# Order of copies, casts and held products in a decoder trunk on one core

## The chip, the cores and the metric

The kernel runs on one core of a Trainium2 chip. The metric is the device time of the whole kernel in microseconds (us), as the median of several runs. The core's engines are named as in the profile: PE (TensorE, matmuls; PEld is its weight load), DVE (VectorE), ACT (ScalarE), POOL (GpSimd) and SP (SyncE, which here only issues transfers).

## What is computed

A two-layer decoder trunk on 512 tokens with 16 learned ones put in front: 528 tokens of width 1024 in float32. Layer 0 mixes with retention (four heads), layer 1 with gated linear attention (GLA, four heads); each mixer stands between two half-step SwiGLU FFNs of inner width 2816.

```python
def rmsnorm(x, g):
    xf = x.astype(jnp.float32)
    y = xf * lax.rsqrt(jnp.mean(xf * xf, axis=-1, keepdims=True) + EPS)
    return (y * g).astype(x.dtype)

def swiglu(x, w_in, w_out):
    gate, up = jnp.split(x @ w_in, 2, axis=-1)
    return (jax.nn.silu(gate) * up) @ w_out
...
    h = jnp.concatenate([meta, x], axis=1)
    for i in range(DEPTH):
        j = i // N_MIXERS
        h = h + 0.5 * swiglu(rmsnorm(h, norm_ffn1[i]), ffn1_w_in[i], ffn1_w_out[i])
...
```

Then the mixer is added (`retention` for i = 0, `gla` for i = 1), then the second FFN, and after both layers a last `rmsnorm` and the first 16 tokens are dropped. `retention` projects to q, k, v and a gate, turns q and k by rotary angles, and runs chunks of 64 tokens with a decaying state.

## The kernel before

**Stages.** The activations stay on the chip, channels on partitions and tokens in two halves of 264. The stages run in turn: FFN f10, retention, FFN f20, FFN f11, GLA, FFN f21. Each FFN has its inner channels in groups: plain gate and up products of a few channels first (tiles `pf20g`, and so on), then per pair of inner tiles a gate unit `g` and an up unit `u`, and after each group the out units `o`, which add to the residual `x`.

**A product.** Matrices are split into a high and a low part, and each product of a 128x128 weight block with 264 tokens is three matmuls (`mm3`, L483 to L485): high weight by high activations, high weight by low, low weight by high.

**A unit.** Two output tiles by two token halves are not made with eight block products but with seven, named a11, s1, s2, a12, s4, s3, a22, on sums and differences of weights and activations. Each is 12 matmuls (9 where three gated tiles make a group). Their results land in three PSUM places: X takes a11, s2, s3 and a22 in the order that the unit has, Q takes a12, Z takes s1 and s4 (Q and Z are one tile, `QZ`). ACT copies X or Z away after s1 (L714), a11 (L716) and s2 (L720); after s3 DVE reads X for the result `c22`, after s4 it reads QZ for `row1`, and after a22 it or ACT reads X for `c21`. In a unit called `rqkk` (keys of a retention head) c22 is L1300 and row1 L1297; in an out unit c22 ends with L1037.

**Three orders of the seven.** A unit is by default held: its last product a22 isn't issued with the unit but kept in `W.held`, and runs when the next unit has begun or when `W.get` is asked for something that the plan doesn't have next (`settle`). So s4 stands before s3 and another unit's products before a22. `LAST` is for units that aren't held, with s3 before s4 and a22 at the end. `FIRST` is the order of an FFN's first unit.

```python
    UNIT = ("a11", "s1", "s2", "a12", "s4", "s3", "a22")
    LAST = ("a11", "s1", "s2", "a12", "s3", "s4", "a22")
    FIRST = ("s1", "s2", "a12", "a11", "s4", "s3", "a22")
```

**Weights.** The plan (`plan_ffn`, `plan_ret` and others) lists all weight pieces in order. SP loads them into `raw` and `pair` tiles; POOL issues transfers that add into `pair` (L151, L153). Sums for s2 and s4 are made by DVE (L191, L193). Then each piece is split: ACT casts `whi` (L184), DVE subtracts to get `wlo` (L185). `hook`, called after each of a unit's products, calls `W.fetch`, which splits up to AHEAD = 4 pieces beyond the one taken. The scheduler that sets the engines' final orders may move these further ahead: `urgent` gives what stands in it a head start of 300 instructions, and `issue_after` holds an instruction behind another.

**Activations of an FFN.** `renorm` splits the sums of the normed activations for the first units (`split`, L516, tiles `uhf`, `ulf`); `evac` takes a gate product with L905 (times the norm) and L906 (silu). `hidden` makes the gated tiles' high parts `hf` (L516).

**What a step does, in its order:** the products, `W.free`, `hook`, and only then the copy or the result.

Of the kernel before, what the change touches and what calls it, by code (L numbers as in the profile page):

```python
# [19 lines left out]
KD = D // P  # L20
# [5 lines left out]
NF = 22  # L26
# [42 lines left out]
class Weights:  # L69
# [11 lines left out]
    def __init__(self, tc, ctx, raw_bufs=7, pair_bufs=3, bufs=7):  # L81
        self.nc, self.tc = tc.nc, tc

        self.behind = None
# [75 lines left out]
    def _split(self, upto):  # L160
        V = self.nc.vector
        while self.split < min(upto, len(self.plan)):
# [17 lines left out]
            with ExitStack() as order_:  # L180
                if self.behind and i < self.FRONT:
                    for ins in self.behind:
                        order_.enter_context(self.tc.issue_after(ins.ins))
                act = self.nc.scalar.copy(hi[:, :n], raw)  # L184
                dve = V.tensor_sub(lo[:, :n], raw, hi[:, :n].bitcast(F32))  # L185
                self.newest = act, dve
# [79 lines left out]
def trunk(ctx, tc, a):  # L266
# [30 lines left out]
    def plan_ffn(w_in, w_out, layer, which, last=False, late=False):  # L297
        first = True
        for kind, a_, b_ in ffn_steps(last, late):
# [11 lines left out]
            elif kind == "i":  # L311
                W.add_unit(key, w_in[layer, o], w_in[layer, o + 1], first,
                           last and b_ == LAST_GROUPS[1][0], last or (a_, b_) != ("u", NF - 2))
# [374 lines left out]
    def unit_steps(key, name, order, halves, ks, rhs, places, row1, c22, c21, behind=None, done=None):  # L688
# [8 lines left out]
        def step(q):  # L697
            if not started:
                hold["X"], hold["QZ"], hold["ab"], hold["s"] = places()
            X, QZ, ab, s_ = [hold[i] for i in ("X", "QZ", "ab", "s")]  # L700
            what, into = WITH[q]
            to = {"X": X, "Q": QZ[:, 0], "Z": QZ[:, 1]}
            w = W.get(key + (q,))
            turn = ks(what)
            for k in turn:
                with tc.issue_after(behind.ins) if behind else ExitStack():
                    ends["unit"] = mm3(to[into], *W.at(w, k * P), *rhs(what, k), k == turn[0] and into not in started,
                                       k == turn[-1], skip_group_check=True)
            started.add(into)
            W.free(w)  # L710
            hook()
            with urgent():
                if q == "s1":
                    S.copy(s_[:, 0], to["Z"])  # L714
                elif q == "a11":
                    S.copy(ab[:, int(first)], X)  # L716
                    if first:
                        V.tensor_sub(ab[:, 0], ab[:, 1], s_[:, 1])
                elif q == "s2":
                    S.copy(s_[:, 1] if first else ab[:, 1], X)  # L720
                elif q == "s3":
                    c22(X, s_[:, 0])
                elif q == "s4":
                    row1(ab, QZ)
                elif q == "a22":
                    c21(X)
# [11 lines left out]
    def unit(key, name, halves, ks, rhs, place, row1, c22, c21, behind=None, done=None, hold=True, first=False):  # L738
# [8 lines left out]
        *steps, last = unit_steps(key, name, W.order(key, first, hold), halves, ks, rhs, places, row1, c22, c21, behind, done)  # L747
# [36 lines left out]
    def ffn(which, layer, halves, gcol, u, feed, late=False):  # L784
# [7 lines left out]
        with tc.tile_pool(name=f"h_{me}", bufs=1) as hp, tc.tile_pool(name=f"t_{me}", bufs=1) as tp, \  # L792
# [47 lines left out]
            def renorm():  # L840
                for h, r0, r1 in ((1, a0, a1), (0, a0, a1), (1, b0, b1)):
# [58 lines left out]
            def evac(f, outs):  # L900

                sg = tmp.tile([P, T], F32, tag="sg", name=f"sg{me}{f}")
                with urgent():
                    for o, view in outs["g"]:
                        V.tensor_mul(view(sg), o, view(rb))  # L905
# [73 lines left out]
            def unit_u(f, g, first):  # L979
# [7 lines left out]
                def row1(ab, qz):  # L987
# [3 lines left out]
                    V.tensor_mul(o, o, pair(g[0], halves))  # L991
                    if last:
                        hidden(f, y[0], 0)

# [11 lines left out]
                def done():  # L1006
                    if f < NPL:
                        todo.append((f, y[0]))
                    elif not last:
# [3 lines left out]
                     place_of[0], row1, c22, c21, None, done, not last, first)  # L1013

            def unit_o(gi, d, behind):
# [29 lines left out]
                unit((which, layer, "o", gi, d), f"{me}o{gi}{d}", halves, ks, rhs, place_of[0], row1, c22, c21, behind)  # L1045
# [3 lines left out]
            for n, (kind, a_, b_) in enumerate(steps):  # L1049
# [23 lines left out]
                elif kind == "i":  # L1073
                    if a_ == "g":
                        g = unit_g(b_, first)
                        if todo:
                            with behind(renormed):
                                hidden(*todo.popleft())
                    else:
# [3 lines left out]
                        unit_u(b_, g, first)  # L1083
                    first = False
# [152 lines left out]
    def retention(u, feed):  # L1237
        with tc.tile_pool(name="retp", bufs=1) as rp, tc.tile_pool(name="wmore", bufs=2) as wp, psum_pool(4) as pp:
# [48 lines left out]
            def head(h):  # L1287
                qk = {}

                def rope_pair(s):  # L1290
# [30 lines left out]
                    unit(("rqk", j), f"rqk{s}{h}", HALVES, rows4_odd, rhs_u, place, row1, c22, c21, None, done)  # L1321
# [978 lines left out]
```

## Time and profile before

| | us |
|---|---|
| median of 3 runs | 2027.35 |
| lowest and highest run | 2026.77, 2835.27 |
| profiled execution | 2025.93 |
| its span, first to last instruction | 2024.2 |
| mean granted PE clock in it | 0.998 |

Rows of the profile's groups give engine, operation, tiles (out<-in), count, busy time, mean ns of one, and idle time before with what ended most of it. Rows of a list of waits give what waited, for what, total us, times, the longest. Rows of a timeline give start and duration in us, and in brackets the idle time before and what ended it. Rows of windows give busy time per engine with instruction counts, then the granted clock, DMA share and GB/s. The lines themselves stand in the prediction where they are used.

### The profile page before, as it was taken

Reading aid. Unit: us, or ns where it says so; the run is one execution under the profiler, and the core shown is the slowest. Engines: PE = TensorE matmul, PEld = TensorE weight load, DVE = VectorE, ACT = ScalarE, POOL = GpSimd, SP = SyncE. Lnnn points to the kernel's source line nnn. Section 1 sums busy time; section 2 is a strip of 40 time slices with the busy share of each in tenths; the row PEclk is TensorE's granted clock in tenths of the full one; section 3 lists DMA queues with packets and bytes.
Section 4 is the critical chain, followed back from the end, with each engine's and each line's share of the span. In section 5 each row is a group of like instructions: output and inputs, shape, how many; then the busy total and the mean of one; then the engine's idle time right before and its main releaser. Section 6 shows DMA issues by size and latency. Waiting matters only on the chain.

```text
span 2024.2 us, 43485 instructions
## 1 busy us (share of the span) xinstructions
PE 2000.5 (99%) x16575; PEld 1967.0 (97%) x16575; DVE 1793.7 (89%) x3302; ACT 1192.0 (59%) x2427; POOL 209.9 (10%) x181
## 2 busy tenths in 40 slices
PE   9999999999999999999999999999999999999998
PEld 9999999999999999999999999999999989999998
DVE  8989999978787889989999998999897968999896
ACT  5656566554555465656666665666645545666664
POOL 1011111010101000111111011111001000111110
PEclk9999999999999999999999999999999999999999
DMA  7576877354645532776876477777515341687772
GB/s 228 137 203 172 205 192 183 106 163 119 164 120 147 135 111 74 181 204 159 212 187 166 127 184 192 180 198 177 183 64 126 103 139 58 166 214 179 183 192 68
DMA packets 176113, 318.87 MB, mean 158 GB/s; under 512 B 17568, under 2 KB 40736, under 8 KB 175904
## 3 DMA queue, kind: packets, MB, share of 16 engines
q1 hardware_dynamic: 133856, 237.04, 35.6%
q0 software_dynamic: 40896, 75.51, 23.4%
q10 hardware_dynamic: 1152, 3.55, 0.6%
q8 instruction: 130, 2.13, 0.4%
q14 instruction: 79, 0.65, 0.1%
HBM read 311.76 MB, written 4.26 MB: 156 GB/s over the span
## 4 chain that ended last, share of the span: by engine, by line
PE 80%; DVE 13%; issue 2%; ACT 2%; DMA 1%; POOL 0%; SPq 0%; DVEq 0%; POOLq 0%; ACTq 0%
DVE wlo L185 4%; PE po_r L484 1%; PE po_r L483 1%; PE po_r L485 1%; ACT whi L184 1%; PE lv L1820 1%; PE Xf11u L483 1%; PE Xf21o L483 1%; PE Xf11u L484 1%; PE Xf21o L485 1%; PE Xf11u L485 1%; PE Xf21o L484 1%; PE Xf21u L483 1%; PE Xf11g L484 1%; PE Xf11g L483 1%
## 5 line engine op out<-in xcount | busy, mean ns | idle before, releaser
L184 ACT CAST whi<-raw 128x512 fp32r<-128x512 f32 (+1 forms) x893 | 531.4, 606 | 436.3 <-DVE raw L193 160.7
L185 DVE TENSOR_TENSOR wlo<-raw,whi 128x512 fp32r<-128x512 f32 (+1 forms) x893 | 589.4, 668 | 105.1 <-ACT whi L184 91.1
L184 ACT CAST whi<-pair 128x512 fp32r<-128x512 f32 (+1 forms) x304 | 183.3, 604 | 67.4 <-ACT su L716 10.7
L185 DVE TENSOR_TENSOR wlo<-pair,whi 128x512 fp32r<-128x512 f32 (+1 forms) x304 | 201.3, 663 | 13.2 <-ACT whi L184 12.3
L153 POOL DMA_DIRECT2D pair<-in_f_in x73 | 89.0, 1220 | 713.3 <-DVE wlo L185 331.3
L193 DVE TENSOR_TENSOR raw<-raw,raw 128x512 f32<-128x512 f32 (+1 forms) x146 | 97.3, 667 | 3.3
L191 DVE TENSOR_TENSOR raw<-pair,raw 128x512 f32<-128x512 f32 (+1 forms) x146 | 97.0, 665 | 3.5 <-DVE wlo L185 0.8
L153 POOL DMA_DIRECT2D pair<-in_f_out x44 | 53.5, 1216 | 352.8 <-DVE wlo L185 125.7
L484 PE MATMUL po_r<-ogl,whi 128*128 128x264 f32 x256 | 71.3, 278 | 0.0
L483 PE MATMUL po_r<-ogh,whi 128*128 128x264 f32 x256 | 71.2, 278 | 0.0
L485 PE MATMUL po_r<-ogh,wlo 128*128 128x264 f32 x256 | 71.2, 278 | 0.0
L153 POOL DMA_DIRECT2D pair<-in_ret_in x20 | 24.4, 1222 | 317.7 <-DVE wlo L185 189.8
L965 ACT ACTIVATE gf<-gf 128x528 f32<-128x528 f32 (+1 forms) x36 | 23.2, 644 | 50.2 <-DVE gf L964 50.2
L483 PE MATMUL Xf10o<-hf,whi 128*128 128x264 f32 x176 | 49.5, 281 | 1.0 <-DVE x L1037 0.7
L483 PE MATMUL Xf20o<-hf,whi 128*128 128x264 f32 x176 | 49.2, 280 | 1.0 <-DVE x L1037 0.7
L483 PE MATMUL Xf11o<-hf,whi 128*128 128x264 f32 x176 | 49.2, 280 | 0.3 <-ACT hf L516 0.3
L484 PE MATMUL Xf10o<-hf,whi 128*128 128x264 f32 x176 | 49.1, 279 | 0.0
L484 PE MATMUL Xf20o<-hf,whi 128*128 128x264 f32 x176 | 49.0, 279 | 0.0
L484 PE MATMUL Xf11o<-hf,whi 128*128 128x264 f32 x176 | 49.0, 279 | 0.0
L485 PE MATMUL Xf10o<-hf,wlo 128*128 128x264 f32 x176 | 48.9, 279 | 0.0
L485 PE MATMUL Xf11o<-hf,wlo 128*128 128x264 f32 x176 | 48.8, 278 | 0.0
L485 PE MATMUL Xf20o<-hf,wlo 128*128 128x264 f32 x176 | 48.8, 278 | 0.0
(1182 smaller groups left out, 8605.2 us busy)
## 6 DMA issues: line engine op xcount, KB each, us to landing
raw<-in_f_in SPq DMA_DIRECT2D x277, 256.0 KB, 3.5
pair<-in_f_in SPq DMA_DIRECT2D x150, 256.0 KB, 4.9
pair<-in_f_in POOLq DMA_DIRECT2D x73, 512.0 KB, 7.6
raw<-in_f_out SPq DMA_DIRECT2D x80, 256.0 KB, 3.3
raw<-in_ret_in SPq DMA_DIRECT2D x76, 256.0 KB, 2.9
raw<-in_f_out SPq DMA_DIRECT2D x72, 192.0 KB, 3.0
pair<-in_f_out SPq DMA_DIRECT2D x48, 256.0 KB, 4.8
pair<-in_f_out POOLq DMA_DIRECT2D x24, 512.0 KB, 6.0
```

Of the source, the lines that this page charges most:

```text
L153: nc.gpsimd.dma_start(t, aps[2].unsqueeze(1).broadcast_to([P, 2, n]), accum_op=ALU.add)
L184: act = self.nc.scalar.copy(hi[:, :n], raw)
L185: dve = V.tensor_sub(lo[:, :n], raw, hi[:, :n].bitcast(F32))
L191: V.tensor_add(s2, self.tiles[c][:, 1], self.tiles[c, "a11"])
L193: V.tensor_add(raw, raw, s2)
L483: nc.tensor.matmul(ps, lhsT=lh, rhs=rh, start=start, stop=False, **kw)
L484: nc.tensor.matmul(ps, lhsT=lh, rhs=rl, start=False, stop=False, **kw)
L485: return nc.tensor.matmul(ps, lhsT=ll, rhs=rh, start=False, stop=stop, **kw)
L965: S.activation(o, o, AF.Silu, scale=-1.0)
L1820: nc.tensor.matmul(ps[:, j, J * P:J * P + n], lhsT=Kt[:, j, J * P:(J + 1) * P], rhs=q, start=(J == 0), stop=(J == 3), skip_group_check=True)
```

## The change

No operation is added or removed; only orders change, in four parts.

**Unheld units ahead of plain products.** The last out unit of f10, f20 and f11 (`feed` given, d = KD - 2 in the last group), the last up unit of f21, and the k units of retention's heads 1 to 3 run in the order LAST, with a22 at their own end. The plan gives the weights in that order too.

**Copies ahead of casts.** For s1, a11 and s2 the copy is now issued before `hook`, and the casts and subtractions of that fetch are held behind the copy (`W.after`).

**First units.** All splits of `renorm` but the first pair stand behind DVE's last product of the gate (`ends["sg"]`), but not in f10 (`late`); the first `hidden` stands behind the copies.

**First out unit of the last group, in two parts.** a11 and s1 run with all gated tiles but the newest, then a11 and s1 with the newest (`parted`).

The core of the diff:

```diff
+                if self.after:
+                    order_.enter_context(self.tc.issue_after(self.after.ins))
                 act = self.nc.scalar.copy(hi[:, :n], raw)
...
                 if kind == "o":
-                    W.add_unit(key, w_out[layer, b_, :, c], w_out[layer, b_ + 1, :, c], False, last and a_ == 0, True)
+                    W.add_unit(key, w_out[layer, b_, :, c], w_out[layer, b_ + 1, :, c], False, last and a_ == 0,
+                               last or (a_, b_) != (len(GROUPS) - 1, KD - 2))
...
-                    W.add_unit(("rqk", j), a["ret_in"][j], a["ret_in"][j + 1], hold=True)
+                    W.add_unit(("rqk", j), a["ret_in"][j], a["ret_in"][j + 1], hold=j < 8)
...
+            if part is not None:
+                late = max(turn)
+                turn = [k for k in turn if k != late] if part == 0 else [late]
...
+        def step(q, part=None):
+            products(q, part)
+            if part == 0:
+                return
+            if q in ("s1", "a11", "s2") or final and q == "s4":
+                W.after = results(q)
+                if first:
+                    ends["copy"] = W.after
+                hook()
+                W.after = None
+            else:
+                hook()
+                results(q)
             if q == "a22" and done:
                 done()
...
+        if parted:
+            (q0, q1), rest = order[:2], order[2:]
+            return [lambda q=q, part=part: step(q, part) for part in range(2) for q in (q0, q1)] + \
+                [lambda q=q: step(q) for q in rest]
         return [lambda q=q: step(q) for q in order]
...
-                        renormed[:] = split(*u.block(k, k + 2, int(r0 == b0)), normed[j][:, :, 1 - h, r0:r1])
+                        with behind([ends["sg"]] if n and not late else []):
+                            renormed[:] = split(*u.block(k, k + 2, int(r0 == b0)), normed[j][:, :, 1 - h, r0:r1])
...
                         if todo:
-                            with behind(renormed):
+                            with behind(renormed + ([ends["copy"]] if first else [])):
                                 hidden(*todo.popleft())
...
                 unit((which, layer, "i", "u", f), f"{me}u{f}", halves, rows4, rhs_in,
-                     place_of[0], row1, c22, c21, None, done, not last, first)
+                     place_of[0], row1, c22, c21, None, done, f + 2 != NF, first, last)
...
-                unit((which, layer, "o", gi, d), f"{me}o{gi}{d}", halves, ks, rhs, place_of[0], row1, c22, c21, behind)
+                unit((which, layer, "o", gi, d), f"{me}o{gi}{d}", halves, ks, rhs, place_of[0], row1, c22, c21, behind,
+                     hold=not feed or (gi, d) != (len(groups) - 1, KD - 2),
+                     parted=bool(feed) and (gi, d) == (len(groups) - 1, 0))
```

What it does to the engines' instructions is shown at three places; line numbers are those of each kernel's own text, and the number behind a name tells tiles apart.

At the first unit of f20, ACT's queue before the change (`su` is the place of the unit's copies, from `QZf20u` after s1 and from `Xf20u` after s2):

```order
L184 CAST whi430_11063<-raw227_10717 128x512
L184 CAST whi431_11082<-pair90_10148 128x512
L516 CAST uhf20_10316<-unf200_10679 128x2x264
L184 CAST whi432_11103<-raw229_10793 128x512
L516 CAST uhf20_10316<-unf201_10825 128x2x264
L906 ACTIVATE sgf203_11032<-sgf203_11032 128x528
L184 CAST whi433_11120<-pair91_10299 128x512
L714 COPY su7_11050<-QZf20u2_11049 128x264
L516 CAST hf200_11301<-unf200_10679 128x3x264
L720 COPY su7_11050<-Xf20u2_11048 128x264
```

The same place after it:

```order
L519 CAST uhf20_10316<-unf200_10679 128x2x264
L519 CAST uhf20_10316<-unf201_10825 128x2x264
L941 ACTIVATE sgf203_11032<-sgf203_11032 128x528
L727 COPY su7_11050<-QZf20u2_11049 128x264
L186 CAST whi430_11064<-raw227_10717 128x512
L734 COPY su7_11050<-Xf20u2_11048 128x264
L186 CAST whi431_11083<-pair90_10148 128x512
L186 CAST whi432_11103<-raw229_10793 128x512
L729 COPY su7_11050<-Xf20u2_11048 128x264
L186 CAST whi433_11122<-pair91_10299 128x512
```

The copy after s1 stood behind the four casts `whi430` to `whi433` and now stands ahead of them, and the activation `sgf` too.

In retention, at the k unit of head 1 on DVE before (`rtk` are the unit's results, `og` and `ogl` the previous head's output, `raq` the first rope product of q):

```order
L185 TENSOR_TENSOR wlo272_6386<-raw136_6005,whi272_6385 128x512
L516 TENSOR_TENSOR ogl0_6157<-og01264_6341,ogh0_6156 128x264
L185 TENSOR_TENSOR wlo273_6421<-raw137_6183,whi273_6420 128x512
L516 TENSOR_TENSOR ogl0_6157<-og02264_6345,ogh0_6156 128x264
L1297 TENSOR_TENSOR rtk10_6308<-su5_6312,QZrqkk1_6311 128x528
L1544 TENSOR_TENSOR og03264_6349<-gs03_5909,bc_ro01_6335 128x264
L1308 TENSOR_TENSOR raq1_6392<-rtq10_6162,ropeq1_6158 128x528
L1300 TENSOR_TENSOR rtk11_6309<-Xrqkk1_6310,su5_6312 128x264
```

And after:

```order
L1585 TENSOR_TENSOR og02264_6346<-gs02_5908,bc_ro01_6336 128x264
L1585 TENSOR_TENSOR og03264_6350<-gs03_5909,bc_ro01_6336 128x264
L187 TENSOR_TENSOR wlo273_6422<-raw137_6184,whi273_6421 128x512
L1340 TENSOR_TENSOR rtk11_6309<-Xrqkk1_6310,su5_6312 128x264
L519 TENSOR_TENSOR ogl0_6157<-og02264_6346,ogh0_6156 128x264
L519 TENSOR_TENSOR ogl0_6157<-og03264_6350,ogh0_6156 128x264
L1348 TENSOR_TENSOR raq1_6392<-rtq10_6162,ropeq1_6158 128x528
L1337 TENSOR_TENSOR rtk10_6308<-su5_6312,QZrqkk1_6311 128x528
```

The read of X (`rtk11<-Xrqkk1`) came last and now stands ahead of the read of QZ and of the rope product. On PE, s4 (into QZ) now stands between s3 and a22 (both into X), where nine matmuls of the plain products `po_r00` stood.

At the first out unit of f10's last group, PE before (`hf1014`, `hf1016`, `hf1018` are gated tiles, `hf1020` is the newest; `whi198` and `whi199` are the weights of a11 and s1):

```order
L483 MATMUL Xf10o20_4411<-hf1018_4152,whi198_4330 128x264
L484 MATMUL Xf10o20_4411<-hf1018_4152,whi198_4330 128x264
L485 MATMUL Xf10o20_4411<-hf1018_4152,wlo198_4331 128x264
L483 MATMUL QZf10o20_4412<-hf1016_3867,whi199_4347 128x264
L484 MATMUL QZf10o20_4412<-hf1016_3867,whi199_4347 128x264
L483 MATMUL Xf10o20_4411<-hf1020_4372,whi198_4330 128x264
L485 MATMUL QZf10o20_4412<-hf1016_3867,wlo199_4348 128x264
L483 MATMUL QZf10o20_4412<-hf1014_3582,whi199_4347 128x264
L484 MATMUL QZf10o20_4412<-hf1014_3582,whi199_4347 128x264
L485 MATMUL QZf10o20_4412<-hf1014_3582,wlo199_4348 128x264
```

And after:

```order
L486 MATMUL QZf10o20_4412<-hf1014_3582,whi199_4347 128x264
L487 MATMUL QZf10o20_4412<-hf1014_3582,whi199_4347 128x264
L488 MATMUL QZf10o20_4412<-hf1014_3582,wlo199_4348 128x264
L486 MATMUL QZf10o20_4412<-hf1018_4152,whi199_4347 128x264
L487 MATMUL QZf10o20_4412<-hf1018_4152,whi199_4347 128x264
L488 MATMUL QZf10o20_4412<-hf1018_4152,wlo199_4348 128x264
L486 MATMUL Xf10o20_4411<-hf1020_4368,whi198_4330 128x264
L487 MATMUL Xf10o20_4411<-hf1020_4368,whi198_4330 128x264
L488 MATMUL Xf10o20_4411<-hf1020_4368,wlo198_4331 128x264
L486 MATMUL QZf10o20_4412<-hf1020_4368,whi199_4347 128x264
```

Before, the newest tile came in the midst of s1 (and products of the next out units were drawn between); now all nine matmuls of s1 with the other tiles come first, and then the newest with both.

More of the change, by code (lines that the diff above doesn't have):

```diff
@@ L82, in __init__ @@
         self.nc, self.tc = tc.nc, tc
-        self.behind = None
+        self.behind = self.after = None
         self.raw_pool = ctx.enter_context(tc.tile_pool(name="wraw", bufs=raw_bufs))
@@ L312, in plan_ffn @@
                 W.add_unit(key, w_in[layer, o], w_in[layer, o + 1], first,
-                           last and b_ == LAST_GROUPS[1][0], last or (a_, b_) != ("u", NF - 2))
+                           last and b_ == LAST_GROUPS[1][0], (a_, b_) != ("u", NF - 2))
                 first = False
@@ L686, in trunk, with unit_steps, products @@
     ends = {}
-    def unit_steps(key, name, order, halves, ks, rhs, places, row1, c22, c21, behind=None, done=None):
+    def unit_steps(key, name, order, halves, ks, rhs, places, row1, c22, c21, behind=None, done=None, final=False,
+                   parted=False):
         started, hold = set(), {}
         first = order == W.FIRST
-        def step(q):
+        def products(q, part):
             if not started:
                 hold["X"], hold["QZ"], hold["ab"], hold["s"] = places()
-            X, QZ, ab, s_ = [hold[i] for i in ("X", "QZ", "ab", "s")]
+            X, QZ = hold["X"], hold["QZ"]
             what, into = WITH[q]
             to = {"X": X, "Q": QZ[:, 0], "Z": QZ[:, 1]}
-            w = W.get(key + (q,))
+            if part != 1:
+                hold[q] = W.get(key + (q,))
+            w = hold[q]
             turn = ks(what)
+            if part is not None:
+                late = max(turn)
+                turn = [k for k in turn if k != late] if part == 0 else [late]
             for k in turn:
@@ L736, in rows4_odd, with unit @@
         return range(4) if what[0] == "n" and what != "n3" else ODD
-    def unit(key, name, halves, ks, rhs, place, row1, c22, c21, behind=None, done=None, hold=True, first=False):
+    def unit(key, name, halves, ks, rhs, place, row1, c22, c21, behind=None, done=None, hold=True, first=False,
+             final=False, parted=False):
         wd = width(halves)
@@ L745, in places @@
             return X, QZ, su[:, :2], su[:, 2:]
-        *steps, last = unit_steps(key, name, W.order(key, first, hold), halves, ks, rhs, places, row1, c22, c21, behind, done)
+        *steps, last = unit_steps(key, name, W.order(key, first, hold), halves, ks, rhs, places, row1, c22, c21,
+                                  behind, done, final, parted)
         for st in steps:
@@ L840, in renorm @@
             def renorm():
-                for h, r0, r1 in ((1, a0, a1), (0, a0, a1), (1, b0, b1)):
+                for n, (h, r0, r1) in enumerate(((1, a0, a1), (0, a0, a1), (1, b0, b1))):
                     for j in range(2):
                         k = 4 * h + 2 * j
-                        renormed[:] = split(*u.block(k, k + 2, int(r0 == b0)), normed[j][:, :, 1 - h, r0:r1])
+                        with behind([ends["sg"]] if n and not late else []):
+                            renormed[:] = split(*u.block(k, k + 2, int(r0 == b0)), normed[j][:, :, 1 - h, r0:r1])
             def gates(f):
@@ L904, in evac @@
                     for o, view in outs["g"]:
-                        V.tensor_mul(view(sg), o, view(rb))
+                        ends["sg"] = V.tensor_mul(view(sg), o, view(rb))
                     S.activation(sg[:, a0:], sg[:, a0:], AF.Silu)
@@ L990, in row1 @@
                     V.tensor_add(o, ab, qz)
-                    V.tensor_mul(o, o, pair(g[0], halves))
+                    ins = V.tensor_mul(o, o, pair(g[0], halves))
                     if last:
                         hidden(f, y[0], 0)
+                    return ins
                 def c22(c, s):
@@ L1083, in ffn @@
                         unit_u(b_, g, first)
+                        if first:
+                            renormed.append(ends["copy"])
                     first = False
@@ L1320, in rope_pair @@
                     j = (0 if s == "q" else 8) + 2 * h
-                    unit(("rqk", j), f"rqk{s}{h}", HALVES, rows4_odd, rhs_u, place, row1, c22, c21, None, done)
+                    unit(("rqk", j), f"rqk{s}{h}", HALVES, rows4_odd, rhs_u, place, row1, c22, c21, None, done,
+                         hold=s == "q")
                 def rope(s):
```

22 lines of the change are left out of this document (13 added, 9 removed).

## The prediction

> **What bounds the kernel now.** I read the page's list of engines first, then the chain of waits, then the waits of TensorE (PE) alone.
>
> ```profile
> span 2024.2 us, 43485 instructions
> PE 2000.5 (99%) x16575; PEld 1967.0 (97%) x16575; DVE 1793.7 (89%) x3302; ACT 1192.0 (59%) x2427; POOL 209.9 (10%) x181
> PE 80%; DVE 13%; issue 2%; ACT 2%; DMA 1%; POOL 0%; SPq 0%; DVEq 0%; POOLq 0%; ACTq 0%
> ```
>
> PE is busy for 2000.5 of 2024.2 us. The change leaves the amount of work alone, so what it can win is part of the 23.7 us in which PE stood still, and what each restart costs beside that. The profiled execution took 2025.93 us (span 2024.2), 1.4 below the median of 2027.35; the sum is made against 2025.93 and the 1.4 is added at the end.
>
> The next fence is from PE's list of waits: total us, times, longest.
>
> ```profile
> PE Xrqkk L483 <- DVE rtk L1300: 1.9, 3, 0.9
> PE st_n L616 <- DVE sqa_n L587: 1.1, 1, 1.1
> ...
> PE QZf20u L483 <- ACT su L714: 1.0, 1, 1.0
> PE pq L483 <- ACT uhret L569: 0.9, 1, 0.9
> PE pg_gz L1708 <- ACT whi L1701: 0.9, 1, 0.9
> ...
> PE Xf10o L483 <- DVE x L1037: 0.7, 1, 0.7
> PE Xf20o L483 <- DVE x L1037: 0.7, 1, 0.7
> ...
> PE QZf11u L483 <- ACT su L714: 0.4, 1, 0.4
> PE Xf10g L483 <- ACT su L720: 0.4, 1, 0.4
> ...
> PE QZf10g L483 <- ACT su L714: 0.2, 1, 0.2
> ```
>
> These are single events at the seams between stages, none over 1.1 us. They are of four kinds, and each part of the change aims at one. A wait costs more than its entry. Here are PE's rows at the first out unit of f10, the first FFN:
>
> ```profile
> 304.81 0.28 PE L483 MATMUL QZf10o<-hf,whi 128*128 128x264 f32 x1
> 304.93 0.28 PE L484 MATMUL QZf10o<-hf,whi 128*128 128x264 f32 x1
> 305.54 0.39 PE L483 MATMUL Xf10o<-hf,whi 128*128 128x264 f32 x1 [0.32 <-ACT hf L516]
> ...
> 307.40 0.39 PE L483 MATMUL QZf10o<-hf,whi 128*128 128x264 f32 x1 [0.39 <-ACT whi L184]
> ```
>
> Running matmuls start 0.12 us apart (304.81, 304.93). The next starts 0.61 later, so 0.49 is lost where the list says 0.32: about 0.16 for the restart on top. I price each wait at its entry plus 0.16, and check that below on the k unit.
>
> **Term 1: k units of retention run unheld (three heads).** A unit is seven products of 12 or 9 matmuls; a22, the last into bank X, was kept back until the first plain product called.
>
> ```profile
> 454.30 0.28 PE L485 MATMUL po_r<-ogh,wlo 128*128 128x264 f32 x1
> 455.03 0.39 PE L483 MATMUL Xrqkk<-rth,whi 128*128 128x264 f32 x1 [0.45 <-DVE rtk L1300]
> ...
> 453.93 0.70 DVE L1308 TENSOR_TENSOR raq<-rtq,ropeq 128x528 f32<-128x528 f32 x1
> 454.55 0.42 DVE L1300 TENSOR_TENSOR rtk<-Xrqkk,su 128x264 f32<-128x264 f32 x1
> ```
>
> Before a22 may write X, DVE reads it for c22 (L1300), which starts at 454.55 behind the unrelated L1308. PE lost 455.03 - 454.30 - 0.12 = 0.61 us, the 0.45 of the row and 0.16. The three together: 1.9 + 3 x 0.16 = 2.4. In the new order 12 matmuls of s4 (12 x 0.12 = 1.4 us) stand between X's last write and a22, and on DVE the read of X moves ahead of both halves of that pair of rope steps; but two other DVE operations (L185's 0.67 and one like L1300's 0.42) still stand in front. Ends: all 2.4 gone, or none (DVE late by 1.4 more). I take 0.25 left of each: **gain 1.6**.
>
> **Term 2: copies ahead of casts, and splits behind the gate, in a first unit.** In f20, the row of PE and ACT's rows before it:
>
> ```profile
> 798.90 0.39 PE L483 MATMUL QZf20u<-uhf,whi 128*128 128x264 f32 x1 [0.99 <-ACT su L714]
> ...
> 797.42 0.64 ACT L906 ACTIVATE sgf<-sgf 128x528 f32<-128x528 f32 x1 [0.42 <-DVE sgf L905]
> 797.97 0.60 ACT L184 CAST whi<-pair 128x512 fp32r<-128x512 f32 x1
> 798.48 0.37 ACT L714 COPY su<-QZf20u 128x264 f32<-128x264 f32 x1
> ...
> 794.43 2.55 DVE L516 TENSOR_TENSOR ulf<-unf,uhf 128x528 fp32r<-128x528 f32 x4
> 796.91 0.42 DVE L905 TENSOR_TENSOR sgf<-pf20g,rb 128x264 f32<-128x264 f32 x1
> ```
>
> PE needs the copy L714. That stood behind a cast, the cast behind the activation, and the activation behind DVE's last gate product at 796.91, which stood behind 2.55 us of splits. Both moves take something from this chain: of the four splits only the first pair stays ahead, and the cast goes behind the copy (about 0.5). The sum of 1.27 from splits (half of 2.55) and 0.5 exceeds 0.99, so the wait goes: 0.99 + 0.16. In f11 it is 0.4 + 0.16. In f10 the two waits of the gate unit (0.4, 0.2, and 2 x 0.16: 0.9) come early, and there the second copy stays behind a cast that waits for DVE; I take 0.4. Ends: 0 and 2.6. **Gain 1.15 + 0.55 + 0.4 = 2.1.** The splits that are moved still come before the next unit's products, which the running matmuls cover; if that cover fails, up to 1.3 us of DVE shows in each first unit.
>
> **Term 3: last out units unheld (the ends of f10, f20, f11).** Before, a22 came between the next stage's plain products. In the list above: at f10's end x L1037 0.7 and uhret 0.9; at f20's end x L1037 0.7; at f11's end whi L1701 0.9 and sqa_n 1.1. The two on x L1037 are of the held kind (the unit's a22 may write X only when c22, L1037, has read it) and go: 2 x 0.86 = 1.7. Those on uhret, whi and sqa_n, 2.9 + 3 x 0.16 = 3.4, are work that the next stage does after the last residual is ready; a22 gives its result earlier by the plain products that stood ahead of it, and so do they, but the same products no longer run meanwhile. A few tenths remain of that; I take 0.4. **Gain 2.1.** Ends: -1.7 (the norm shows by as much as the two waits were) and +5.1.
>
> **Term 4: the first out unit in two parts (f10, f20, f11).** Its first two products wait for the newest gated tile and for a cast behind it: 0.32 and 0.39, with 0.16 each 1.03; the other two FFNs have like rows (0.3 and 0.4):
>
> ```profile
> PE QZf11o L483 <- ACT whi L184: 0.4, 1, 0.4
> ...
> PE QZf20o L483 <- ACT whi L184: 0.4, 1, 0.4
> ...
> PE Xf11o L483 <- ACT hf L516: 0.3, 1, 0.3
> ...
> PE Xf20o L483 <- ACT hf L516: 0.3, 1, 0.3
> ```
>
> So 3.1 in all. With all other tiles of both products first, 18 matmuls (2.1 us) run before the newest tile, where 11 ran. But the change makes a new wait: a11's last matmul into X now has only s1's last three behind it before s2 writes X.
>
> ```profile
> 309.66 0.28 PE L485 MATMUL Xf10o<-hf,wlo 128*128 128x264 f32 x1
> 309.98 0.38 ACT L720 COPY szf<-Xf10o 128x264 f32<-128x264 f32 x1 [0.28 <-PE Xf10o L485]
> ```
>
> A copy starts 0.32 after the last matmul's start and takes 0.38: X is free after 0.70, and the three matmuls plus one step give 4 x 0.12 = 0.47. A wait of 0.25, with its restart 0.4, replaces 1.03. **Gain 3 x 0.63 = 1.9**; ends 0 (ACT is late for that copy by 0.7 more) and 3.1.
>
> **Term 5: casts later.** Casts of a fetch now wait for the copy, so weights are split some three to five tiles ahead of PE where up to seven were; raw and pair tiles come free later, and the loads on SP's queue and the pair sums that POOL issues move with them.
>
> ```profile
> 900.00:925.00 25.00, 25.00 (x217) 25.00 (x216) 22.42 (x39) 15.49 (x32) 3.65 (x3) 1.00 0.69 190
> L184 ACT CAST whi<-raw 128x512 fp32r<-128x512 f32 (+1 forms) x893 | 531.4, 606 | 436.3 <-DVE raw L193 160.7
> L185 DVE TENSOR_TENSOR wlo<-raw,whi 128x512 fp32r<-128x512 f32 (+1 forms) x893 | 589.4, 668 | 105.1 <-ACT whi L184 91.1
> POOL pair L153 <- DVE wlo L185: 678.1, 61, 44.1
> ```
>
> The window is a plain stretch of f20 (us, then PE, PEld, DVE, ACT, POOL busy): PE full, DVE with 2.6 us to spare in 25, ACT with 9.5. A split takes 0.61 + 0.67 = 1.3 us and three tiles last PE 3 x 1.4 = 4.2, so the shorter lead still covers it. POOL stands waiting for 678 us in one row alone, which covers its issues. Only where DVE is behind (stage seams) can a tile be late: three new waits of the smallest kind listed (0.2 + 0.16) give **-1.0**; ends 0 and -3.
>
> **Term 6: the clock.** PE's granted clock stands after the five busy times:
>
> ```profile
> 1433.61:1436.73 3.12, 2.03 (x18) 1.81 (x17) 2.29 (x6) 0.96 (x2) 0.14 (x1) 1.00 1.06 344
> 1436.73:1440.14 3.41, 3.41 (x18) 3.41 (x17) 2.49 (x6) 1.23 (x2) 1.78 (x2) 0.50 1.08 273
> ```
>
> Right after the 1.1 us wait at GLA's norm the clock is 0.50 for 3.41 us: half of that, 1.7 us, is lost. I keep it (0); ends +1.7 (gone) and -1.7 (another). [...]
>
> **Sum.** 1.6 + 2.1 + 2.1 + 1.9 - 1.0 = 6.7 us. 2025.93 - 6.7 = 2019.2, and 1.4 for the median: **2020.6 us**.
>
> **Rivals.** First, the gains come to nothing: in every seam DVE's backlog is the real limit, as in the row of L1308 ahead of L1300, and waits only change their names. DVE's 89% speaks for it, that ACT is what PE waits for in most rows against. Time: 2027, within 3.
>
> Second, all targeted waits go: 2.4 + 2.6 + 5.1 + 3.1 = 13.2, so about 2014. Against it: PE's list also holds data that no reordering brings sooner.
>
> Third, the other side: a copy that must wait for PE's last matmul now stands ahead of the casts in ACT's queue, so casts, wlo and the matmuls behind them come later in every unit, not only in seams.
>
> ```profile
> L191 DVE TENSOR_TENSOR raw<-pair,raw 128x512 f32<-128x512 f32 (+1 forms) x146 | 97.0, 665 | 3.5 <-DVE wlo L185 0.8
> ```
>
> There are 146 units (L191 runs once in each). A copy in front delays the next cast by up to the 0.32 + 0.38 above. Break-even is 6.7 / 146 = 0.05 us of PE a unit; 0.2 a unit gives 2020.6 + 29 = 2050, and 2% is passed from (40.5 + 6.7) / 146 = 0.32. Against it are the 9.5 us of 25 that ACT has free. [...]
>
> Fourth, one or two more stretches of half clock at seams that now gap differently: 2020.6 + 1.7 to 3.4, about 2023; or the one of before gone, 2018.9.
>
> **How the numbers follow.** Chances: forecast, with its own range 2015.5 to 2024.5, 0.50; nothing 0.20; all gone 0.12; casts held, slower than before 0.12; clock more or less than that 0.06. Half of "all gone" and of the clock case, the forecast and nearly all of "nothing" make 0.8: 2012 to 2029. About 2% (40.5 us) is what a measurement of this kernel can tell from no change. Faster by more than that, below 1986.8, would need more than PE's whole idle time: 0.01. Slower by more, above 2067.9, is the third rival at its strong end: 0.03. Within: 0.96.
>
> **What would show it.** Term 1: the entry Xrqkk on rtk falls below 0.6 in all. Term 2: no QZf20u wait on a copy. Term 3: no x L1037 among PE's waits; uhret and sqa_n a little shorter. Term 4: hf and whi go from the out units, and s2's matmul waits about 0.25 on the copy of a11 in three FFNs. Term 5: PE still full in the stretch of f20. The forecast is wrong if PE's idle time stays above 21 us, or if waits on wlo or whi turn up inside the units.

## The result

The change made the kernel slower by about 1%, where 0.3% faster was forecast.

| | before | after |
|---|---|---|
| median of 6 runs, us | 2027.06 | 2045.93 |
| lowest | 2023.74 | 2042.73 |
| ratio to before (95% interval) | | 1.0096 [1.0080, 1.0113] |
| profiled execution, us | 2025.93 | 2050.43 |
| its span, us | 2024.2 | 2048.6 |

The profiled execution after is the slowest of its six, so its spans overstate the median by some 4.5 us. The interval lies clear of 1, though the change is within the 2% that the prediction took for what a measurement can tell. From the page after, the span, the engines and the chain that ended last:

```profile
span 2048.6 us, 43376 instructions
PE 2011.0 (98%) x16575; PEld 1971.2 (96%) x16575; DVE 1785.1 (87%) x3302; ACT 1182.1 (58%) x2427; POOL 209.8 (10%) x181
PE 74%; DVE 17%; ACT 3%; issue 2%; DMA 2%; POOL 0%; SPq 0%; ACTq 0%; DVEq 0%; POOLq 0%
```

PE has the same 16575 records. It stood still for 2048.6 - 2011.0 = 37.6 us, against 23.7, and its busy time is 10.5 us longer: 3.4 of that is two more stretches at half clock (term 6 below), and the restarts behind more waits are in it too, which were not summed. The list of PE's waits after (total us, times, longest) shows where:

```profile
PE pg_gz L1749 <- ACT whi L1742: 3.1, 1, 3.1
PE Xrqkk L486 <- ACT su L734: 2.0, 2, 1.1
PE pf11g L486 <- ACT uhf L572: 1.6, 1, 1.6
PE st_n L619 <- DVE sqa_n L590: 1.4, 1, 1.4
PE pq L486 <- ACT uhret L572: 1.4, 1, 1.4
PE Xrqkk L488 <- DVE wlo L187: 1.3, 1, 1.3
...
PE po_r L486 <- DVE rtk L1337: 1.1, 1, 1.1
...
PE QZf11o L486 <- ACT whi L186: 0.8, 1, 0.8
PE QZf20o L486 <- ACT whi L186: 0.8, 1, 0.8
PE QZf10o L486 <- ACT whi L186: 0.8, 1, 0.8
...
PE QZf10o L488 <- DVE wlo L187: 0.4, 1, 0.4
```

Gone, as forecast: the waits on rtk before a22 (Xrqkk), on x L1037 and on the first unit's copy (QZf20u, QZf11u). But the stage entries (pq, pf11g, pg_gz) wait longer than before, the keys' units wait for another thing, and the first out units wait for weights (whi, wlo). In nearly all of these ACT or DVE is late with a split, of a weight or of an activation (`uhf`, `uhret`). Inside the FFNs nothing is lost, as the window of f20 shows that answers to the one shown before (us, then PE, PEld, DVE, ACT, POOL, the clock, DMA share, GB/s):

```profile
912.00:937.00 25.00, 25.00 (x217) 25.00 (x216) 23.35 (x42) 14.96 (x31) 2.42 (x2) 1.00 0.76 203
```

**How far ahead the casts run.** PE ran 10.33 us later at this place, so 910.33 after is the same matmul as 900.00 before. Windows from the start to there, of the casts alone (ACT busy and their number), before first and after second:

```profile
0.00:900.00 900.00, 300.15 (x506) 1.00 0.59 157
...
0.00:910.33 910.33, 292.66 (x503) 1.00 0.58 155
```

506 casts done against 503. Counted so at 80 points (every 200th matmul of PE's order), the kernel after is 1.6 casts behind the one before on average (1.7 over all matmuls), mostly by 2 to 4 inside the FFNs. This count is called the lead below.

**What it does at a seam.** ACT after, at f10's first out unit (start, us, operation, idle before):

```profile
306.34 0.38 ACT L727 COPY szf<-QZf10o 128x264 f32<-128x264 f32 x1
307.58 0.41 ACT L519 CAST hf<-t1f10h 128x264 fp32r<-128x264 f32 x1 [0.86 <-DVE t1f10h L908]
307.92 0.38 ACT L734 COPY szf<-Xf10o 128x264 f32<-128x264 f32 x1
310.15 0.62 ACT L186 CAST whi<-raw 128x512 fp32r<-128x512 f32 x1 [1.85 <-DVE raw L195]
...
310.82 0.40 PE L486 MATMUL QZf10o<-hf,whi 128*128 128x264 f32 x1 [0.78 <-ACT whi L186]
```

The copies are on time. No weight was cast between them; the next cast waits 1.85 us for DVE's sum L195, because it comes only now that DVE is busy with gated tiles, and PE (last row) waits for that cast. The chain of waits between 1440 and 1458 us, the entry of GLA, shows the longer way (start, us, what):

```profile
1443.83 0.70 DVE wlo L187
1444.52 0.02 issue
1444.54 7.57 DMA raw<-in_gla_in
1452.11 0.02 issue
1452.13 0.02 ACTq L186
1452.15 0.04 issue
1452.19 0.62 ACT whi L186
1452.81 0.65 ACT uhgla L572
```

A `wlo` that ends late frees its raw tile late, the load into it starts late (1444.54) and lands 7.57 us on, and ACT's cast stands at the head of ACT's queue until then. The next stage's scaling `uhgla`, which doesn't need this weight, stands behind it.

### The profile page after: what moved, and what is told of

The parts are those of the page before. It is cut to its first block, busy times and chain, and to the rows that moved or that the text cites. A ratio compares the mean times of both kernels' runs of the same rounds, so it can differ in the third digit from the quotient of the medians.

```text
span 2048.6 us, 43376 instructions
## 1 busy us (share of the span) xinstructions
PE 2011.0 (98%) x16575; PEld 1971.2 (96%) x16575; DVE 1785.1 (87%) x3302; ACT 1182.1 (58%) x2427; POOL 209.8 (10%) x181
## 4 chain that ended last, share of the span: by engine, by line
PE 74%; DVE 17%; ACT 3%; issue 2%; DMA 2%; POOL 0%; SPq 0%; ACTq 0%; DVEq 0%; POOLq 0%
DVE wlo L187 5%; PE po_r L488 1%; PE po_r L487 1%; PE po_r L486 1%; ACT whi L186 1%; DVE hf L519 1%; PE lv L1861 1%; PE Xf21o L486 1%; PE Xf21o L488 1%; PE Xf21o L487 1%; DVE raw L195 1%; DVE raw L193 1%; PE Xf21u L486 1%; PE Xf21g L486 1%; PE Xf21u L488 1%
## 5 line engine op out<-in xcount | busy, mean ns | idle before, releaser
L195 DVE TENSOR_TENSOR raw<-raw,raw 128x512 f32<-128x512 f32 (+1 forms) x146 | 97.3, 666 | 2.8
L486 PEld LDWEIGHTS po_r<-ogh,whi 128*128 128x128 f32 x256 | 48.6, 190 | 2.1 <-issue 1.3
L486 PE MATMUL Xf20o<-hf,whi 128*128 128x264 f32 x176 | 49.6, 282 | 0.1
L486 PE MATMUL Xf10o<-hf,whi 128*128 128x264 f32 x176 | 49.6, 282 | 0.1
L487 PEld LDWEIGHTS po_r<-ogl,whi 128*128 128x128 f32 x256 | 48.5, 190 | 0.7 <-DVE ogl L519 0.7
```

The costliest lines, as they stand in the source:

```text
L195: V.tensor_add(raw, raw, s2)
L486: nc.tensor.matmul(ps, lhsT=lh, rhs=rh, start=start, stop=False, **kw)
L487: nc.tensor.matmul(ps, lhsT=lh, rhs=rl, start=False, stop=False, **kw)
```

## The experiments

Two theories to begin with. H1, late casts: the hold of casts behind copies is the loss. H2, cover lost: the new order of the products is (a22 no longer covers the ends of stages, and the out unit in two parts has no fetch between). All ratios are to the kernel before, on the same chip, with 95% intervals.

**Undo one part, or do one alone.** First the hold: the changed kernel with

```diff
-            if q in ("s1", "a11", "s2") or final and q == "s4":
-                W.after = results(q)
-                if first:
-                    ends["copy"] = W.after
-                hook()
-                W.after = None
-            else:
-                hook()
-                results(q)
+            hook()
+            ins = results(q)
+            if first and q in ("s1", "a11", "s2"):
+                ends["copy"] = ins
```

> The changed kernel with the old order of copy and cast (the fetch first, then the copy, nothing held behind a copy); unheld units, splits behind the gate and the unit in two parts stay. Theory H1 (late casts): casts held behind copies shorten the lead, raw tiles come free later, and casts then stand at the head of ACT's queue waiting for transfers or sums, with copies and the next stage's splits behind them; that is most of the 19 us. It expects 2022 to 2030, and ACT's casts waiting for transfers no longer than before the change. Theory H2 (cover lost): the loss lies in the products' new order (a22 no longer covers the stage ends, two products of the out unit with no fetch between). It expects 2040 or more, with the waits for uhret, uhf, whi L1742 at the stage ends as long as after the change.

Measured: 2025.05 us, 0.9994 [0.9985, 1.0004]. H1's number. The kernel with the copies written ahead of the fetch but nothing held (`W.after` alone left out) has the same order of instructions on PE, DVE and ACT as this one, so the hold is the whole of that part: `urgent` had put the copies ahead already where it could.

Then the change without the two parts:

```diff
-                     parted=bool(feed) and (gi, d) == (len(groups) - 1, 0))
+                     parted=False)
```

> The changed kernel with the first out unit in one piece as before; the rest of the change stays. The waits in and right behind the three first out units come to about 3 us each after the change and 1.05 each before. H2 expects 6 us back (2040). H1 expects that these waits come from casts that are late anyway: 0 to 3 us back (2043 to 2046), with waits on whi or wlo still in these units.

Measured: 2044.73, 1.0089 [1.0073, 1.0105]: nothing back that can be told. In this run's profile the waits of the first out units are those of after, 0.8 on whi and 0.5 on wlo in each of the three, so they were casts that are late anyway.

Then all units held as before:

```diff
-                    W.add_unit(("rqk", j), a["ret_in"][j], a["ret_in"][j + 1], hold=j < 8)
+                    W.add_unit(("rqk", j), a["ret_in"][j], a["ret_in"][j + 1], hold=True)
...
-                     hold=not feed or (gi, d) != (len(groups) - 1, KD - 2),
...
-                     place_of[0], row1, c22, c21, None, done, f + 2 != NF, first, last)
+                     place_of[0], row1, c22, c21, None, done, not last, first, last)
```

> The changed kernel with all units held as before (out units, keys' units of retention, last up unit of f21); copies, splits and the two parts stay. H2 expects that the stage ends go back to 2.4, 1.3 and 2.3 us from about 3.5, 3.6 and 4.8 and the keys' units to 2.4 from about 6: some 10 us back (2036). H1 expects under 4 us back (2042 to 2046), since casts stay late, with new waits at the a22 that are kept back.

Measured: 2038.71, 1.0058 [1.0044, 1.0072]: 7 us back, between the two theories. Beside the hold the unheld units do cost; without it (the first run) they don't.

Last, the hold alone on the kernel before:

> The kernel before with one part of the change alone: copies ahead of the fetch and casts held behind them. H1 expects 2040 to 2047, nearly all of the loss. H2 expects 2022 to 2028, no loss or a small gain from copies that come earlier.

Measured: 2042.11, 1.0070 [1.0056, 1.0084]: 15 of the 19 us. H1 holds for the most part; H2's part needs the hold.

**Is it the lead, or the copy that blocks the queue?** The changed kernel with one number changed:

```diff
-AHEAD = 4
+AHEAD = 6
```

> The changed kernel with fetches that go 6 instead of 4 pieces beyond the one taken; the hold behind copies stays. Counted at 80 points of PE's order, the change had 1.6 casts fewer done than before, on average, and nothing of that without the hold. Theory H1a (the short lead is what costs): with two more pieces asked for, a tile or more of the lead comes back and the time with it, 2026 to 2035. Theory H1b (the copy itself blocks: it waits in ACT's queue for PE's last matmul and everything behind it waits too, however early it was asked for): the lead comes back in part but the time stays above 2040.

Measured: 2034.98, 1.0037 [1.0024, 1.0050]. The lead is 0.4 below before instead of 1.6, and more than half of the loss is back. The same with 8:

> The changed kernel with fetches that go 8 pieces beyond the one taken; the hold and all else stays. With 6 the mean count of casts done at PE's points was 0.4 below that of before, and the loss 8 of 19 us. H1a expects the lead back in full (0.2 below or less) and the time at 2024 to 2032. If the hold costs something that no lead gives back (a copy that blocks), the time stays at 2033 to 2037 with the lead restored.

Measured: 2031.15, 1.0016 [1.0007, 1.0024]; the lead is that of before (0.03 above on average). Of 19 us 3 are left, with every copy still ahead of its casts. In this profile the entry of GLA and the first out unit of f20 read:

```profile
PE pg_gz L1749 <- ACT whi L1742: 0.6, 1, 0.6
...
PE Xf20o L488 <- DVE wlo L187: 0.4, 2, 0.2
```

3.1 has become 0.6. So the lead carries the loss and the copy at the queue's head does not, but for the 3 us at most. Even these need not be the copy's: this profile's span is 7.0 us longer than that of before, and ahead of the kernel's end it has two stretches at half clock of 6.83 us, which cost 3.4 each, where before has one of 3.41 us, which cost 1.7:

```profile
21.76:28.59 6.83, 6.83 (x30) 6.56 (x31) 2.72 (x7) 0.00 (x0) 3.48 (x3) 0.50 0.85 213
1438.27:1445.10 6.83, 6.83 (x32) 6.83 (x33) 3.62 (x9) 1.85 (x3) 1.92 (x2) 0.50 0.81 199
```

One rival is left open: no run has the longer fetch without the hold. If it would win something there too, part of the 16 us is a gain of the fetch and not the lead given back.

The other way about, the kernel before with a shorter fetch, AHEAD = 2:

> The kernel before with fetches that go 2 instead of 4 pieces beyond the one taken; nothing is held behind a copy. H1a expects a shorter lead and with it a loss of the size that the change had, 2033 to 2050, at the same seams (first out units, stage ends, retention). H1b expects 2025 to 2030, since no copy blocks.

Measured: 2031.94, 1.0022 [1.0013, 1.0032]. This run doesn't tell: its lead did not fall (it is within 0.05 of before), which I put down to the scheduler's pulling casts ahead on its own, and 6.8 us of its 9.7 us of longer span stand in the first 56 us, where two plain products of f10 wait for a cast:

```profile
PE pf10g L483 <- ACT whi L184: 5.4, 2, 4.6
```

Taking a buffer away does shorten the lead. The kernel before with

```diff
-    def __init__(self, tc, ctx, raw_bufs=7, pair_bufs=3, bufs=7):
+    def __init__(self, tc, ctx, raw_bufs=7, pair_bufs=3, bufs=6):
```

> The kernel before with six instead of seven buffers for split weights: nothing is held, the casts can only be one piece less ahead. If the lead is what counts (H1a), casts done fall by about 1 at PE's points inside the FFNs and the time rises by 3 to 10 us (2030 to 2037), with waits on whi or wlo at the same seams. If a lead of six is as good as seven: 2025 to 2029.

Measured: 2031.07, 1.0023 [1.0012, 1.0034], with a lead 0.55 lower at the 80 points (0.76 over all matmuls). New waits on wlo and whi stand in the same out units, with no hold and no changed order anywhere:

```profile
PE Xf10o L485 <- DVE wlo L185: 0.6, 1, 0.6
PE Xf11o L485 <- DVE wlo L185: 0.6, 1, 0.6
PE Xf20o L485 <- DVE wlo L185: 0.6, 1, 0.6
```

By PE's starts these units cost 0.75 us each more than before, 2.3 in all. This profile's span is 7.5 us longer, and its mean granted clock is 0.996 against 0.998; over 2031.6 us that is some 4 us more lost to the clock (an estimate from the two rounded figures), so the size of this loss is less sure than its place.

**Where does the hold cost?** The changed kernel with the hold on one set of units:

```diff
-                W.after = results(q)
+                ins = results(q)
+                seam = name[0] != "f" or name[3:5] == "o2"
                 if first:
-                    ends["copy"] = W.after
+                    ends["copy"] = ins
+                if not seam:
+                    W.after = ins
```

> The changed kernel with the hold behind copies kept in the gate and up units and in the out units of the FFNs' earlier groups, and taken away in the out units of the third group (the last but in f21) and in the mixers. The traces place the loss at the first out units of the last group, the stage ends and in retention. If the hold costs only there (theory S, seams): 2024 to 2030, though casts inside the FFNs stay 2 to 4 behind. If a unit pays for the hold wherever it is (the third rival of the prediction): 2034 or more, as most of the 146 units keep it.

Measured: 2037.62, 1.0054 [1.0041, 1.0067]. And with `if seam:`

> The other half: the hold only in the out units of the FFNs' third group and in the mixers. S expects most of the 19 us, 2036 to 2046. The third rival expects a part by the number of units, about a third or half: 2030 to 2036.

Measured: 2039.09, 1.0062 [1.0049, 1.0074]. Theory S is wrong as I put it: a hold inside the FFNs costs 12 us, and that is the number which the expectation gave to the third rival. Yet the cost stands at the seams. In the profile of the first of the two, PE is full in f20 and the waits are those of the seams:

```profile
866.00:891.00 25.00, 25.00 (x217) 25.00 (x215) 20.44 (x37) 12.27 (x25) 3.65 (x3) 1.00 0.70 199
...
PE pg_gz L1752 <- ACT whi L1745: 2.1, 1, 2.1
...
PE pq L486 <- ACT uhret L572: 1.2, 1, 1.2
...
PE QZf10o L486 <- ACT whi L186: 0.8, 1, 0.8
```

By PE's starts against those of before, this profile loses 3.7, 4.3 and 2.8 us in f10, f20 and f11 from the last group's first out unit to the next stage's first products, units that have no hold in this run; in the long stretch of gate, up and earlier out units ahead of them, where the hold stands, f20 gains 0.3 and f11 loses 0.5. The lead is lost in one place and missed in another, and its mean is no price: 0.4 below before goes with 13 us in the second run here and with 8 us at AHEAD = 6. Retention goes the other way: from the values' first unit in head 1 to the entry of f20, the kernel with the hold in the mixers fell 6.0 us further behind the kernel before; the one without it there gained 0.3. The two kernels' losses (12 and 13) add up to more than the 19; that each alone makes the same seams wait would explain it, but was not tested.

**Unheld units.** Held as before and AHEAD = 6, beside 2034.98 with unheld ones:

> The changed kernel with all units held as before and fetches 6 pieces beyond; the hold behind copies stays. With fetches of 4 the held units were worth 7 us (2039 against 2046). If unheld units lose only because the casts are late (no a22 left to cover them), then with the lead mostly back held or unheld makes no difference: 2033 to 2037, as with unheld units and 6 pieces. If unheld units lose of themselves once anything is held behind copies: 2026 to 2030.

Measured: 2034.56, 1.0035 [1.0023, 1.0047]. No difference any more: unheld units lose only where splits come late and a22 isn't there to cover them.

**What the rest of the change is worth.** Without the hold, and with f21's last up unit held as before:

> The changed kernel without the hold, and with f21's last up unit held as before. In the profile of the kernel without the hold the only loss against before stands at that unit's a22 (a wait of 1.2 us on DVE's read of X, 1.4 with its restart). If that is so the time falls by 1 to 2 us against the kernel without the hold: 2022.5 to 2024.5, the whole interval below the kernel before. If the losses there only cover others at the same place: 2025, as without the hold.

Measured: 2025.96, 0.9995 [0.9986, 1.0004]. With the hold in first units only, beside that:

> As the one before (f21's last up unit held), and with the hold behind copies in an FFN's first unit only, where the copy stood behind casts (waits of 0.7 us in f20 and f11 without any hold). H1a expects the two waits to go and little else, since three pieces held once per FFN change the lead only there: 2021 to 2023. H1b, or a lead that is needed at just that place: 2024 or more, with new waits on whi or wlo in the first units.

Measured: 2026.84, 0.9999 [0.9991, 1.0008]. And with unheld units and the two parts alone on the kernel before:

> The kernel before with the two parts of the change that took PE's waits away when nothing was held behind copies: unheld out units and keys' units, and the first out unit in two parts. Splits behind the gate, the hold and f21's unheld unit are left out. By the waits in the profile without the hold, these two take some 3 us at the ends of f10, f20, f11 and in retention: 2022.5 to 2024.5, a ratio of about 0.9985, which should lie below 1 with its whole interval. If what is gained is lost again at the next wait, or to a stretch of half clock, 2025 to 2027.

Measured: 2025.97, 0.9994 [0.9985, 1.0003]. All three are the same as before by their intervals, and the gains that their expectations put first (2022.5 to 2024.5, 2021 to 2023, and 2022.5 to 2024.5) did not come. I found no version that is faster than the kernel before by more than the measurement's doubt; three of them, with the first run, lie 1.3 to 1.7 us below it.

## Why the prediction was wrong

**Term 5 failed, casts later: -1.0 was forecast, some -20 measured** (2045.93 with the hold, 2025.05 without). The forecast held that a split of 1.3 us is covered by a lead of three tiles, 4.2 us, and by the spare time in a plain stretch of f20. That is true of the stretch: PE is full there after as before. But the lead is spent at the seams, where ACT and DVE are taken up with gated tiles, norms and rope: at f10's first out unit one cast waited 1.85 us for DVE. The step named the second round (raw tiles come free later and the loads move with them) and gave it no price: at GLA's entry one such load landed 7.57 us after its tile was free. Its -1.0 was three waits of the smallest kind in a list that showed only what a long lead leaves over. A list of waits prices what is missing now, not what a buffer covers.

**The third rival** had the right sign and, in a wider sense, the right engine, with a chance of 0.12, and 2050 us is near the 2045.93. But its mechanism is not borne out: it put a delay of the next cast in every unit, and 146 units that each pay 0.13 us would show in the plain stretches, where next to nothing is lost. The hold inside the FFNs alone came out at that rival's number (2037.62, where 2034 or more was put down to it), but its loss stands behind the units that have the hold. With the lead restored the copies still stood ahead and 16 of 19 us were back. What ACT's queue cost stands in a place I had not looked for, behind a cast that waits for its load: the last of the matmuls that the copy at 454.59 below reads started at 452.52, but the copy starts only in the last 0.10 us of the cast ahead of it (454.07 and 0.62 us long), which had waited 1.05 us; and the scaling `uhgla` at GLA's entry, whose last part of `x` DVE had written by 1448.21, came at 1452.81, behind the cast that waited.

**The price of a restart was too low.** The prediction took 0.16 beside a wait's entry. Its own rows go on:

```profile
305.76 0.29 PE L485 MATMUL QZf10o<-hf,wlo 128*128 128x264 f32 x1
```

The matmul behind the one that waited starts 0.22 after it (305.54), not 0.12, so 0.11 more is lost; over 23 waits of more than 0.2 us at L483 in the kernel before the medians are 0.16 and 0.11. The price is 0.27; with it alone mended the forecast would have been larger, and further off.

**Term 1, the keys' units: 1.6 forecast, 0.9 without the hold, a loss of 4.5 with it (1.7 of that is a stretch at half clock).** Without the hold the list of PE's waits has, in place of 1.9 us on rtk:

```profile
PE Xrqkk L486 <- ACT su L734: 0.9, 2, 0.5
```

A third of 0.1 is too small for the list; with 0.27 a wait, the three before cost 2.7 and these 1.8. The mechanism was right, c22's read is out of the way. The step looked only at who reads X before a22, not before s3: in the order LAST, s3 stands where s4 stood, with only a12's twelve matmuls after s2, and waits for the copy of s2. After, with the hold, that copy stood behind a cast that waited for its transfer:

```profile
454.07 0.62 ACT L186 CAST whi<-raw 128x512 fp32r<-128x512 f32 x1 [1.05 <-DMA raw<-in_ret_o]
454.59 0.37 ACT L734 COPY su<-Xrqkk 128x264 f32<-128x264 f32 x1
```

**Term 2, first units: 2.1 forecast.** After, the two waits on the copy went as forecast: from f20's first up unit to its next gate unit the kernel gained 1.4 us on the one before, in f11 0.9. But it takes the hold: without it casts stood ahead of the copy again, and both waits were 0.7 (1.0 and 0.4 before), so 0.3 was gained in f20 and 0.2 lost in f11. In f10 0.5 was gained in the gate unit, where 0.4 was forecast, and 0.8 lost in the up unit behind it, which waited for its weights (whi 0.3, wlo 0.2).

**Term 3, ends of stages: 2.1 forecast, about 1.2 without the hold** (f10 1.3, f20 0.2, f11 -0.3, each from PE's starts against its cadence). The waits on x L1037 shrank to 0.3 us and a small one on ACT's copy came beside them; at f11's end the wait for sqa_n grew from 1.1 to 1.8. With the hold this term turned into the largest loss.

**Term 4, the first out unit: 1.9 forecast, 0.05 in each of the three without the hold, some 0.1 in all** (from PE's starts on both sides of the unit). The waits on hf went from the list; one of 0.4 on a later cast stayed in each FFN. But the newest tile's products then start 0.23 us apart instead of 0.12, twice, with no idle time that the list could show, and a12 starts 0.28 late behind s2, so that some 1.2 us are lost in such a unit as before (1.35). With the hold, the wait that I put against the term, on X behind a11's copy, is 0.07 in the list and 0.35 by PE's starts; 0.4 was forecast. The step read the list as if a wait that leaves it were time won.

**Left out of the sum:** f21's last up unit. Without the hold its a22 waits 1.2 us for DVE's read of X (the entry Xf21u on su L1029), so that 1.5 went back with the late starts behind it. With this unit held as before, the same read still cost it 0.6, so only part came back. The terms without the hold are then 0.9 + 0.1 + 1.2 + 0.1 - 1.5 = 0.8 us of gain. The measured 1.7 (2025.05 against 2026.72), itself inside the doubt, does not confirm that sum: the profile of this run has a mean granted clock of 0.999, against 0.998 in the one of before with its half clock behind GLA's norm, 1.7 us in itself, and its span is only 1.5 us shorter (2022.7 against 2024.2). So the order has gained nothing there that can be told from the clock.

**Term 6, the clock: kept at 0, it cost 3.4 in the profiled run.** Three stretches before the kernel's end run at half clock, against one:

```profile
664.26:667.67 3.41, 3.41 (x17) 3.15 (x16) 3.41 (x7) 1.03 (x3) 0.00 (x0) 0.50 0.88 228
1111.41:1114.82 3.41, 3.41 (x16) 3.30 (x15) 3.21 (x5) 1.02 (x2) 0.00 (x0) 0.50 0.86 161
1500.53:1503.94 3.41, 3.41 (x18) 3.41 (x17) 3.41 (x9) 0.53 (x2) 0.00 (x0) 0.50 0.20 67
```

Each follows waits of PE shortly before it: 1.1 and 1.3 (po_r on rtk, Xrqkk on wlo; the second ends 0.86 us before the stretch), 1.6 and 0.4 (pf11g on uhf and ulf; 0.32 before), and 1.1 alone (gv on vt; 0.61 before). Each costs 1.7 us, half of 3.41; in the last, matmuls start 0.22 us apart instead of 0.12. This is what the fourth rival named, as a part of the loss and not the whole.

## What to carry to other kernels

Here the lead of the casts over PE was a stock, spent at the seams; what shortening it cost showed at the seams (3.7, 4.3 and 2.8 us with the hold inside the FFNs), not where it was shortened (0.3 gained in f20, 0.5 lost in f11). Before casts, loads or copies are tied to one another, count how far ahead they run at the places where their engine is busy with other things, and look at what is queued behind an instruction that waits for a transfer. When a change in order loses, give the lead back by itself (a longer fetch, one more buffer) before judging the rest: here a longer fetch brought 16 of 19 us back with all else unchanged. Run the longer fetch without the change too, which is missing here.

## What the runs showed of the hardware

One load of a raw tile took 7.57 us from its release to its landing at the entry of GLA, where the core's DMA moved 340 GB/s; the 43 loads of these tiles take 3.0 us in the median (last row: KB each, us to landing):

```profile
1444.00:1458.00 14.00, 9.41 (x76) 8.83 (x75) 8.70 (x15) 7.31 (x15) 1.22 (x1) 1.00 1.07 340
...
raw<-in_gla_in SPq DMA_DIRECT2D x43, 256.0 KB, 3.0
```

And PE's clock stood at half for 3.41 us behind some waits of little over 1 us and not behind others: the wait of gv on vt is 1.1 us in the kernel before (its matmul at 1479.96) and after (at 1499.92), and only after does half clock follow it (0.50 from 1500.53, against 1.00 from 1440.14 on, past that wait, before). None followed the longest wait after, the 3.1 us of pg_gz that ended at 1450.57 (1.00 in the window above). What decides between the two cases was not tried. Behind a wait PE lost 0.16 us at the matmul that had waited and 0.11 at the next, beside the wait itself (medians of the 23 waits of more than 0.2 us at L483 in the kernel before; 305.54 and 305.76 are the two matmuls of one).
